# Order of weight sums, squares into PSUM, a last column block in two parts and closer turns in a one-core transformer block

## The chip, the cores and the metric

The kernel runs on one core of one Trainium2 chip. The core has TensorE (PE) for matmuls, VectorE (DVE), ScalarE (ACT), GpSimd (POOL) and SyncE (SP), which mostly issues DMAs. The metric is the device time of one execution in microseconds (us), taken as a median of several executions. A profile of one execution shows what each engine did and when.

## The reference

One layer on 256 tokens of width 2048, batch 1, all in fp32:

```
u = rms_norm(x);  z = u @ w_in          # 2048 -> hq hf hi hg | aq ak av | two gates
y_a = hgrn2_scan(silu(hq), 1-g, hi, log g), g = lb + (1-lb)*sigmoid(hf)   # 8 heads of 128, chunks of 64
y_a = rms_norm(y_a) * silu(hg)
y_b = attention over a band of 9 chunks with a relative bias              # 16 heads of 64
m = sigmoid(ga) * (y_a @ w_branch_a) + sigmoid(gb) * (y_b @ w_branch_b)
h = x + m @ w_out                       # 2048 x 2048
h = h + relu(rms_norm(h) @ w_up)**2 @ w_down   # 2048 -> 8192 -> 2048
out = rms_norm(h)
```

## The kernel before

**Matmuls.** Each fp32 product is three matmuls in a reduced form (`mm3`, L142 to L145): high part of the left times high part of the weight (L143), high times low (L144), low times high (L145). A weight piece of 128 x 1024 fp32 (512 KB) is loaded raw by SP (`piece`, L716), cast by ACT to its high part `wh` (L89) and subtracted by DVE to give the low part `wl` (L90). So PE waits for ACT and then DVE on each piece. A right-hand side has 512 columns at most; a PSUM bank holds 512 fp32 columns.

**HGRN stage.** The projections hf and hq are computed transposed (`gemm_t`, L171), the chunks hi and hg directly (`gemm`, L162). Beside these the small work of the recurrence is threaded through a list `behind` of steps with distances: each pass over a block of 128 rows of weights calls `tick` (L152), with 1 in `gemm_t` and 2 in `gemm`, and when the head step's distance is used up it is issued. `scores` (L517) puts eight steps per pair of heads on the list, the first of which, `diagonal`, makes the products `ps` (L373) from `q` (written by DVE at L338); its distance for pair 0 is 12. `group` (L535) puts on the list the outputs and then the turns of two pairs, the latter with distance `gap2`. A turn (`finish`, L491 on) transposes an output block on PE into a PSUM tile `tpo` (L493; the pool has two buffers), then ACT casts it and DVE subtracts (both into `act_ya`). The last step of attention's preparation before `ak` is `aq00T` (L193).

**Units.** Gates, output projection and the MLP run in units of 1024 output columns, two blocks of 512 (n = 0 and 1), for two row halves m: `Unit` (L758) and `run` (L854). The first half of the reduction is done with seven products of sums in place of eight (raw pieces A, B, C, D, each two tiles; sums of weights are made in place: A+B and A+C by DVE in `sums`, L816; B+C and D+A by accumulating DMAs from POOL in `sent`, L821). The sums of the left side, S2, S4, S5, S7, come from `combos` (L658; DVE at L679 to L685, then a split by ACT and DVE). The second half is plain pieces (`ITEMS`, L756). The last two pieces of column block 1 (`LATE`, k = 12, 13 and 14, 15) run inside the next unit, called by `q()` in `run`: one behind the next unit's first product, one behind its second. Names: `wl_wo2r` is the low part of a plain piece of unit wo2, `wl_up00p22A` that of piece A (by then A+B) in product 22 of unit up00. The units in order are ga2, gb0, gb2, (branch products), wo0, wo2, and then up00, up02, dn00, dn02 and so on to dn32.

**Order.** The scheduler of the framework puts each engine's instructions in an order of its own from the order in which they are written, with work under `high_priority` pulled ahead; what waits for what follows from buffers.

**Between wo2 and up00** `h_out` (L1031) adds x to the result; `h_blocks` (L1002) transposes it (`tp_h`, on PE at L106, in a pool of two PSUM buffers), multiplies by the norm's weight into `hw` (DVE, L1013), splits that into `act_h`, and takes the squares of h on ACT with a sum along the row (`hsq`, L1015) into a scratch tile in SBUF, a `token`; POOL's loads of x into such tokens (L1034) wait for tokens to come free.

**The end.** `out_of` (L1076) adds the result to h (`evict`, L753), takes squares on ACT (L1086), and with the last column block sums the squares, makes rstd (DVE L95, POOL L96), scales four blocks of 512 columns (i = 0 and 1 on ACT, 2 and 3 on DVE) and stores them, even i by ACT's queue, odd i by SP's.

Of the kernel before, what the change touches and what calls it, by code (L numbers as in the profile page):

```python
# [50 lines left out]
def tile_hybrid_block(  # L51
# [90 lines left out]
    def mm3(acc, hi, lo, wh, wl, first, last):  # L142
        nc.tensor.matmul(acc, hi, wh, start=first, stop=False, skip_group_check=True)  # L143
        nc.tensor.matmul(acc, hi, wl, start=False, stop=False, skip_group_check=True)  # L144
        nc.tensor.matmul(acc, lo, wh, start=False, stop=last, skip_group_check=True)  # L145
# [13 lines left out]
    def later(*steps):  # L159
        behind.extend([n, f] for n, f in steps)  # L160
# [356 lines left out]
    def scores(n, made, gap, first=None, between=()):  # L517

        sc = []
        steps = []  # L520

        def one(i):
            if not i:
                out, fs = hgrn_scores(n, made)
                sc.extend(out)
                steps.extend(fs)
            steps[i]()

        todo = [(gap if i or first is None else first, lambda i=i: one(i)) for i in range(8)]
        for at, f in between:  # L530
            todo.insert(at, (gap, f))
        later(*todo)
        return sc
# [13 lines left out]
    a0, a1 = fq(0), fq(1)  # L547
    a0[1]()
    a0[2]()
    s0 = scores(0, a0[0], 5, 12, ((5, a1[1]), (8, a1[2])))  # L550
    vs0 = v_chunk(0)
    s1 = scores(1, a1[0], 4)
    gws0 = hg_chunk(0)
# [6 lines left out]
    vs1 = v_chunk(1)  # L560
    s3 = scores(3, a3[0], 4)
    gws1 = hg_chunk(1)
    later(*group(1, s2, s3, vs1, gws1, 2, 3))
    acc_q = [gemm_t(xT, w_in_t, C_AQ + i * T, KD, f"aq0{i}") for i in range(2)]
    while behind:
        tick(9)
# [191 lines left out]
    class Unit:  # L758
# [64 lines left out]
        def plain(self, n, ks, which=range(NM)):  # L823

            while self.steps and self.steps[0][0] <= ks[-1] // 4:
                self.steps.pop(0)[1]()
            if (n, ks) not in self.raw:
                self.load_item()
            wh, wl = parts(self.raw[n, ks], f"{self.what}r{n}_{ks[0]}")

            def half(m):
                for a, k in enumerate(ks):
                    mm3(self.c["12"[m] + "12"[n]], *lhs_of(self.lhs(), k, m), wh[:, a], wl[:, a], False, k == KD - 1)

            for m in which:
                half(m)
            return half
# [16 lines left out]
    def run(u, then=None):  # L854

        def q():
            if late:
                late.pop(0)()

        def item(x):  # L860
            if x and x.items:
                x.load_item()

        if not u.raw:
            u.load("A")
            u.load("B")
            u.load("C")
            u.load("D")
        for _ in range(3 - sum(type(k) is tuple for k in u.raw)):
            item(u)  # L870
        at = iter(range(99))
        u.bank("11")
        u.product("11", "A", u.block(0, 0), True)
        u.sums("A", "B")
        u.begun("21", "11")
        u.sent("B", "C")
        q()
        item(u)
        u.bank("22")
        u.product("22", "A", u.comb(5), True)  # L880
        u.begun("12", "22")
        q()
        item(u)
        u.steps = list(u.make_steps())
        u.step(next(at))
        u.product("12", "C", u.comb(4))
        u.sums("A", "C")
        u.step(next(at))
        u.product("11", "D", u.block(0, 1))
        u.sent("D", "A")  # L890
        u.step(next(at))
        u.plain(1, (8, 9))
        item(u)
        u.step(next(at))
        u.product("21", "A", u.comb(2))
        u1 = u.copy(token(f"u1_{u.what}"), "21")
        if then:
            then.load("A")
        u.step(next(at))
        u.plain(1, (10, 11))  # L900
        u.less("12", u1)
        item(u)
        u.step(next(at))
        u.product("21", "B", u.comb(7))
        u2 = u.copy(token(f"u2_{u.what}"), "21")
        if then:
            then.load("B")
            then.load("C")
        u.step(next(at))
        u.plain(0, (8, 9))  # L910
        u.less("22", u2)
        item(u)
        u.step(next(at))
        u.plain(0, (10, 11))
        item(u)
        u.step(next(at))
        u.product("21", "D", u.block(1, 1))
        if then:
            then.load("D")
        u.step(next(at))  # L920
        u.plain(0, (12, 13))
        item(u)
        u.step(next(at))
        u.plain(0, (14, 15))
        item(then)
        u.end(0)
        while u.steps:
            u.step(99)

        if u.tail:  # L930
            halves = [u.plain(1, ks, ()) for ks in LATE]
            for m in range(NM):
                for h in halves:
                    h(m)
                u.done(m, 1, u.c["12"[m] + "2"])
            return

        def rest():
            u.plain(1, LATE[1])
            u.end(1)  # L940

        late.append(lambda: u.plain(1, LATE[0]))
        late.append(rest)
# [58 lines left out]
    def h_blocks(n0):  # L1002

        def one(n, m):
            if not m:
                hT.append(new_act(f"h{n}"))
            hi, lo = hT[n][:, :, 0, :], hT[n][:, :, 1, :]
            t = h1[n][m]
            tp = transpose4(t, f"h{n}{m}")
            tmp = fours(token(f"hw_{n}_{m}"))  # L1010
            hw[m, n] = tmp
            with tc.high_priority(offset=2000):
                nc.vector.tensor_tensor(tmp, tp, bc(wmlp[:, 4 * n:4 * n + 4], 2, P), op=ALU.mult)  # L1013
                split(hi[:, :, m * P:(m + 1) * P], lo[:, :, m * P:(m + 1) * P], tmp)
            nc.scalar.activation(token(f"hsq_{n}_{m}"), t, AF.Square, accum_out=ssq2[:, m, n:n + 1])  # L1015

        def factor():
            ssum2 = small.tile([P, NM], F32, name="ssum2", tag="ssum")
            nc.vector.tensor_reduce(ssum2, ssq2, axis=AX.X, op=ALU.add)
            rsqrt(rstd2, ssum2, D, NM)  # L1020

        def soon(f):
            with tc.high_priority(offset=2000):
                f()

        return [(n if n0 else 99, lambda n=n, m=m: one(n, m)) for n in (n0, n0 + 1) for m in range(NM)] + [
            (99, lambda f=f: soon(f), 6) for f in ([factor] if n0 else combos(hT, "h", sp, Sh, hw))]
# [8 lines left out]
        nc.gpsimd.dma_start(hd[n][m], t)  # L1036
        h1[n][m] = t

    ssq3 = small.tile([P, NM, 4], F32, name="ssq3", tag="ssq3")
    ssum3 = small.tile([P, NM], F32, name="ssum3", tag="ssum")  # L1040
    rstd3 = const.tile([P, NM], F32, name="rstd3")
    NQ = 4
# [3 lines left out]
    for qd in range(NQ):  # L1046
# [26 lines left out]
            units.append(Unit(lambda: hT, lambda: Sh, w_up, qd * (FF // NQ) + c * NC, f"up{qd}{c}", done,  # L1073
                              steps=(lambda turns=turns: turns(0)) if c else (lambda: ()) if qd else (lambda: h_blocks(2)), start=3 if c else 0))

        def out_of(m, n, acc, last=last, qd=qd):  # L1076
            if not last:
                t = token(f"y{qd}{n}{m}")
                with tc.high_priority(offset=2000):
                    nc.scalar.copy(t, acc)  # L1080
                nc.gpsimd.dma_start(hd[n][m], t, accum_op=ALU.add)
                return
            wf = fin["w"]
            r = fin[m][:, n * NC:(n + 1) * NC]
            evict(r, acc)
            nc.scalar.activation(token(f"ysq_{n}_{m}"), r, AF.Square, accum_out=ssq3[:, m, n:n + 1])  # L1086
            if n < 3:
                nc.vector.tensor_tensor(r, r, wf[:, n * NC:(n + 1) * NC], op=ALU.mult)
                return
            nc.vector.tensor_reduce(ssum3[:, m:m + 1], ssq3[:, m, :], axis=AX.X, op=ALU.add)  # L1090
            rsqrt(rstd3[:, m:m + 1], ssum3[:, m:m + 1], D, 1)
            f = rstd3[:, m:m + 1]
            for i in range(4):
                t = fin[m][:, i * NC:(i + 1) * NC]
                if i == 3:
                    nc.vector.scalar_tensor_tensor(t, t, f, wf[:, i * NC:(i + 1) * NC], op0=ALU.mult, op1=ALU.mult)
                elif i == 2:
                    nc.vector.tensor_scalar(t, t, f, None, op0=ALU.mult)
                else:
                    nc.scalar.activation(t, t, AF.Copy, scale=f)  # L1100
                (nc.sync if i % 2 else nc.scalar).dma_start(out[m * P:(m + 1) * P, i * NC:(i + 1) * NC], t)

        def finals():
            fin["w"] = apool.tile([P, D], F32, name="wf", tag="act")
# [5 lines left out]

        for n0 in (0, 2):
            units.append(Unit(lambda uT=uT: uT, lambda Su=Su: Su, w_down, n0 * NC, f"dn{qd}{n0}",
                              lambda m, n, acc, n0=n0, out_of=out_of: out_of(m, n0 + n, acc), kt0=qd * KD,
                              steps=(lambda: ()) if n0 else (lambda turns=turns, last=last: turns(2) + [(3, finals)] * last),
                              start=0, tail=last and n0 == 2))

# [46 lines left out]
```

## Time and profile before

| what | value |
|---|---|
| time, median of 3 runs | 1404.46 us (1403.69 to 1406.17) |
| the profiled execution's own time | 1403.92 us |
| its span, first to last instruction | 1402.2 us |
| mean granted TensorE clock | 0.998 |
| busy: PE, DVE, ACT, POOL | 99%, 80%, 65%, 10% of the span |
| moved by DMA | 327.42 MB, 234 GB/s on average |

The rows of the timeline give start and duration in us, engine, line, operation, tiles (out<-in), shape, and in brackets the idle time ahead of it with the instruction that ended it. A row of the waits gives engine, line and tile that waited, who ended the wait, total us, count and the longest. A row of the windows gives the stretch in us, its length, busy us of PE, PE's weight load, DVE, ACT and POOL with the number of instructions, the granted clock, the share of the DMA engines' time and GB/s.

### The profile page before, as it was taken

The numbers are of one execution on the slowest core, as the hardware profiler recorded it, in microseconds if no ns is written. First come the engines' busy times: TensorE is split into PE (matmuls) and PEld (weight loads), VectorE is DVE, ScalarE is ACT, GpSimd is POOL, SyncE is SP. The second block draws the span as 40 slices with busy tenths as digits, with TensorE's granted clock in tenths as the row PEclk, the third lists the DMA queues.
The fourth block names the chain that finished last, engine by engine and source line by source line (L and its number), as shares of the span: only waits on it lengthen the run. The fifth ranks groups of instructions, "written<-read, shape, count | busy, mean of one in ns | idle before, by whom it ended". The sixth has DMA issues, their size and how long they took to land.

```text
span 1402.2 us, 18580 instructions
## 1 busy us (share of the span) xinstructions
PE 1385.6 (99%) x6562; PEld 1149.9 (82%) x6562; DVE 1116.7 (80%) x1406; ACT 909.4 (65%) x1170; POOL 138.6 (10%) x220
## 2 busy tenths in 40 slices
PE   9999999999999999999999999999999999999997
PEld 8889888878787888888878888888888888888885
DVE  7897997675758785687998977889877897878885
ACT  6774754464656664446767876678666876668764
POOL 2000001010000000001211001100011001110200
PEclk9999999999999999999999999999999999999999
DMA  9654455555578987558988889988899888998883
GB/s 326 232 173 157 152 165 162 182 175 170 155 236 267 267 249 238 187 177 263 271 255 274 249 263 270 270 268 246 253 296 291 249 229 256 279 304 258 262 249 118
DMA packets 122925, 327.42 MB, mean 234 GB/s; under 512 B 10944, under 2 KB 11712, under 8 KB 122448
## 3 DMA queue, kind: packets, MB, share of 16 engines
q1 hardware_dynamic: 103264, 264.80, 55.3%
q0 software_dynamic: 18416, 59.84, 21.6%
q10 hardware_dynamic: 1152, 1.60, 0.3%
q8 instruction: 51, 0.84, 0.2%
q14 instruction: 42, 0.34, 0.1%
HBM read 271.67 MB, written 10.49 MB: 201 GB/s over the span
## 4 chain that ended last, share of the span: by engine, by line
PE 93%; DVE 2%; DMA 2%; issue 1%; ACT 1%; POOL 0%; ACTq 0%; POOLq 0%; DVEq 0%
PE acc_ak L185 2%; PE acc_aq L185 2%; PE acc_hf L185 1%; PE ps L417 1%; PE acc_hq L185 1%; PE acc_ga L144 1%; PE tp_u L106 1%; PE acc_ga L145 1%; PE acc_hg L143 1%; PE acc_hg L144 1%; PE acc_bb L143 1%; PE acc_ba L145 1%; PE acc_av L144 1%; PE acc_hg L145 1%; PE acc_ba L143 1%; PE acc_bb L145 1%
## 5 line engine op out<-in xcount | busy, mean ns | idle before, releaser
L185 PE MATMUL acc_hf<-act_x,wh_hf 128*128 128x512 f32 x128 | 46.3, 400 | 0.4 <-DVE f L193 0.4
L185 PE MATMUL acc_aq<-act_x,wh_aq 128*128 128x512 f32 x128 | 46.5, 400 | 0.0
L185 PE MATMUL acc_ak<-act_x,wh_ak 128*128 128x512 f32 x128 | 45.3, 399 | 0.7 <-DVE aq00T L193 0.7
L185 PE MATMUL acc_hq<-act_x,wh_hq 128*128 128x512 f32 x128 | 45.9, 397 | 0.0
L184 PE MATMUL acc_aq<-act_x,wl_aq 128*128 128x256 f32 x120 | 35.3, 294 | 0.0
L90 DVE TENSOR_TENSOR wl_ga<-raw_ga,wh_ga 128x1024 fp32r<-128x1024 f32 x16 | 19.6, 1225 | 19.6 <-ACT wh_ga L89 19.6
L184 PE MATMUL acc_hf<-act_x,wl_hf 128*128 128x256 f32 x120 | 34.3, 286 | 0.0
L184 PE MATMUL acc_hq<-act_x,wl_hq 128*128 128x256 f32 x120 | 34.2, 285 | 0.0
L184 PE MATMUL acc_ak<-act_x,wl_ak 128*128 128x256 f32 x120 | 33.7, 281 | 0.0
L90 DVE TENSOR_TENSOR wl_av<-raw_av,wh_av 128x1024 fp32r<-128x1024 f32 x16 | 19.6, 1224 | 16.7 <-ACT wh_av L89 16.7
L89 ACT CAST wh_bb<-raw_bb 128x1024 fp32r<-128x1024 f32 x16 | 16.8, 1053 | 23.3 <-PE acc_ba L145 17.8
L90 DVE TENSOR_TENSOR wl_bb<-raw_bb,wh_bb 128x1024 fp32r<-128x1024 f32 x16 | 19.6, 1224 | 14.8 <-ACT wh_bb L89 14.8
L89 ACT CAST wh_av<-raw_av 128x1024 fp32r<-128x1024 f32 x16 | 16.8, 1051 | 21.5 <-PE acc_av L145 12.4
L89 ACT CAST wh_ba<-raw_ba 128x1024 fp32r<-128x1024 f32 x16 | 16.8, 1051 | 20.9 <-PE acc_bb L145 13.8
L90 DVE TENSOR_TENSOR wl_aq<-raw_aq,wh_aq 128x1024 fp32r<-128x1024 f32 x16 | 19.6, 1224 | 13.4 <-ACT wh_aq L89 13.3
L90 DVE TENSOR_TENSOR wl_ba<-raw_ba,wh_ba 128x1024 fp32r<-128x1024 f32 x16 | 19.6, 1224 | 12.5 <-ACT wh_ba L89 12.5
L185 PEld LDWEIGHTS acc_ak<-act_x,wh_ak 128*128 128x128 f32 x128 | 24.0, 188 | 6.6 <-DVE aq00T L193 1.0
L89 ACT CAST wh_aq<-raw_aq 128x1024 fp32r<-128x1024 f32 x16 | 16.8, 1047 | 19.1 <-PE acc_hg L145 9.3
L185 PEld LDWEIGHTS acc_hf<-act_x,wh_hf 128*128 128x128 f32 x128 | 24.2, 189 | 5.7 <-DVE f L193 0.7
L185 PEld LDWEIGHTS acc_aq<-act_x,wh_aq 128*128 128x128 f32 x128 | 24.1, 189 | 5.2 <-issue 0.7
L89 ACT CAST wh_ga<-raw_ga 128x1024 fp32r<-128x1024 f32 x16 | 16.8, 1050 | 17.6 <-PE acc_ga L145 10.8
L185 PEld LDWEIGHTS acc_hq<-act_x,wh_hq 128*128 128x128 f32 x128 | 24.1, 188 | 5.0
(1806 smaller groups left out, 5249.9 us busy)
## 6 DMA issues: line engine op xcount, KB each, us to landing
raw_hi<-in_w_in_n_dram SPq DMA_DIRECT2D x16, 512.0 KB, 4.3
raw_hg<-in_w_in_n_dram SPq DMA_DIRECT2D x16, 512.0 KB, 3.8
raw_aq<-in_w_in_t_dram SPq DMA_DIRECT2D x16, 512.0 KB, 4.0
raw_ak<-in_w_in_t_dram SPq DMA_DIRECT2D x16, 512.0 KB, 3.8
raw_av<-in_w_in_n_dram SPq DMA_DIRECT2D x16, 512.0 KB, 4.3
raw_ga<-in_w_in_t_dram SPq DMA_DIRECT2D x16, 512.0 KB, 3.8
raw_ba<-in_w_branch_a_dram SPq DMA_DIRECT2D x16, 512.0 KB, 4.5
raw_bb<-in_w_branch_b_dram SPq DMA_DIRECT2D x16, 512.0 KB, 4.6
```

The lines of the kernel that those rows point to most:

```text
L89: (copy or nc.scalar.copy)(hi, src)
L90: nc.vector.tensor_tensor(lo, src, hi.bitcast(F32), op=ALU.subtract)
L106: nc.tensor.transpose(tp[:, j, :], src[:, j * P:(j + 1) * P], ident)
L143: nc.tensor.matmul(acc, hi, wh, start=first, stop=False, skip_group_check=True)
L144: nc.tensor.matmul(acc, hi, wl, start=False, stop=False, skip_group_check=True)
L145: nc.tensor.matmul(acc, lo, wh, start=False, stop=last, skip_group_check=True)
L184: nc.tensor.matmul(acc[:, cb, 0:T], wl[:, c], r[:, 0, :], start=False, stop=False)
L185: nc.tensor.matmul(acc[:, cb, :], wh[:, c], r.rearrange("p u t -> p (u t)"), start=kt == 0, stop=kt == nkt - 1)
L417: nc.tensor.matmul(ps[:, m, :], klf[:, a * P:(a + 1) * P], qrf[:, a * 192:(a + 1) * 192], start=True, stop=True)
```

## The change

Five edits:

- HGRN: the first diagonal of pair 0 has distance 13 in place of 12, and the turns of group 1 distance 2 in place of 3.
- In each unit the late piece (`q()`) is written ahead of the sum A+B, and the sum A+C behind the product with D.
- The squares of h are written into the PSUM tile of the transposes in place of a token.
- The last column block of the last unit, row half 1, is computed as two blocks of 256 columns, each with its own eviction and squares. The sums of squares get a fifth column.
- The outputs are scaled and stored in the order 2, 0, 3, 1, with 2 and 3 on SP's queue and 0 and 1 on ACT's.

```diff
-    s0 = scores(0, a0[0], 5, 12, ((5, a1[1]), (8, a1[2])))
+    s0 = scores(0, a0[0], 5, 13, ((5, a1[1]), (8, a1[2])))
...
-    later(*group(1, s2, s3, vs1, gws1, 2, 3))
+    later(*group(1, s2, s3, vs1, gws1, 2, 2))
...
-            def half(m):
+            def half(m, c=slice(0, NC)):
                 for a, k in enumerate(ks):
-                    mm3(self.c["12"[m] + "12"[n]], *lhs_of(self.lhs(), k, m), wh[:, a], wl[:, a], False, k == KD - 1)
+                    mm3(self.c["12"[m] + "12"[n]][:, c], *lhs_of(self.lhs(), k, m), wh[:, a, c], wl[:, a, c], False, k == KD - 1)
...
         u.product("11", "A", u.block(0, 0), True)
+        u.begun("21", "11")
+        q()
         u.sums("A", "B")
-        u.begun("21", "11")
         u.sent("B", "C")
-        q()
         item(u)
...
         u.product("12", "C", u.comb(4))
-        u.sums("A", "C")
         u.step(next(at))
         u.product("11", "D", u.block(0, 1))
+        u.sums("A", "C")
         u.sent("D", "A")
...
-            for m in range(NM):
+            for m, c in ((0, slice(0, NC)), (1, slice(0, T)), (1, slice(T, NC))):
                 for h in halves:
-                    h(m)
-                u.done(m, 1, u.c["12"[m] + "2"])
+                    h(m, c)
+                u.done(m, 1, u.c["12"[m] + "2"], c)
...
-            nc.scalar.activation(token(f"hsq_{n}_{m}"), t, AF.Square, accum_out=ssq2[:, m, n:n + 1])
+            nc.scalar.activation(tp.rearrange("p k t -> p (k t)"), t, AF.Square, accum_out=ssq2[:, m, n:n + 1])
...
-            evict(r, acc)
-            nc.scalar.activation(token(f"ysq_{n}_{m}"), r, AF.Square, accum_out=ssq3[:, m, n:n + 1])
+            evict(r[:, c], acc[:, c])
+            j = n + (c.start > 0)
+            nc.scalar.activation(token(f"ysq_{j}_{m}")[:, c], r[:, c], AF.Square, accum_out=ssq3[:, m, j:j + 1])
...
+            if c.stop < NC:
+                return
-            nc.vector.tensor_reduce(ssum3[:, m:m + 1], ssq3[:, m, :], axis=AX.X, op=ALU.add)
+            nc.vector.tensor_reduce(ssum3[:, m:m + 1], ssq3[:, m, 0:j + 1], axis=AX.X, op=ALU.add)
...
-            for i in range(4):
+            for i in (2, 0, 3, 1):
...
-                (nc.sync if i % 2 else nc.scalar).dma_start(out[m * P:(m + 1) * P, i * NC:(i + 1) * NC], t)
+                (nc.sync if i > 1 else nc.scalar).dma_start(out[m * P:(m + 1) * P, i * NC:(i + 1) * NC], t)
```

More of the change, by code (lines that the diff above doesn't have):

```diff
@@ L1037, in h_out @@
         h1[n][m] = t
-    ssq3 = small.tile([P, NM, 4], F32, name="ssq3", tag="ssq3")
+    ssq3 = small.tile([P, NM, 5], F32, name="ssq3", tag="ssq3")
     ssum3 = small.tile([P, NM], F32, name="ssum3", tag="ssum")
@@ L1074, in tile_hybrid_block, with out_of @@
                               steps=(lambda turns=turns: turns(0)) if c else (lambda: ()) if qd else (lambda: h_blocks(2)), start=3 if c else 0))
-        def out_of(m, n, acc, last=last, qd=qd):
+        def out_of(m, n, acc, c=slice(0, NC), last=last, qd=qd):
             if not last:
@@ L1112, in tile_hybrid_block @@
             units.append(Unit(lambda uT=uT: uT, lambda Su=Su: Su, w_down, n0 * NC, f"dn{qd}{n0}",
-                              lambda m, n, acc, n0=n0, out_of=out_of: out_of(m, n0 + n, acc), kt0=qd * KD,
+                              lambda m, n, acc, *c, n0=n0, out_of=out_of: out_of(m, n0 + n, acc, *c), kt0=qd * KD,
                               steps=(lambda: ()) if n0 else (lambda turns=turns, last=last: turns(2) + [(3, finals)] * last),
```

## The prediction

> **What bounds the kernel now.** I read the page first: busy shares, then the chain that ended last.
>
> ```profile
> span 1402.2 us, 18580 instructions
> PE 1385.6 (99%) x6562; PEld 1149.9 (82%) x6562; DVE 1116.7 (80%) x1406; ACT 909.4 (65%) x1170; POOL 138.6 (10%) x220
> PE 93%; DVE 2%; DMA 2%; issue 1%; ACT 1%; POOL 0%; ACTq 0%; POOLq 0%; DVEq 0%
> ```
>
> TensorE (PE) is busy for 1385.6 of 1402.2 us, and 93% of the chain of work that ended last is PE. The change removes no full-rate matmul work, so it can only win gaps: 16.6 us in all, most of them the load at the start and the output at the end. The waits of PE name the gaps inside.
>
> ```profile
> PE acc_wo2c L144 <- DVE wl_wo2r L90: 2.1, 2, 1.1
> PE acc_ga2c L144 <- DVE wl_ga2p11D L90: 1.0, 1, 1.0
> PE acc_ak L185 <- DVE aq00T L193: 0.7, 1, 0.7
> PE ps L373 <- DVE q L338: 0.5, 1, 0.5
> PE tpo L493 <- DVE act_ya L90: 0.4, 1, 0.4
> ```
>
> These five are 4.7 us. The timeline makes each a little longer, since a matmul still counts as busy when the next could have started: full ones start 0.227 us apart (0.23 in the first two rows below), so a gap is what exceeds that. DVE ends every one of the five, so what decides is DVE's order, which here I take from the instruction lists of the two kernels on each engine.
>
> **Part 1, first diagonal of HGRN pair 0 one tick later (12 to 13).**
>
> ```profile
> 60.76 0.39 PE L145 MATMUL acc_hi<-wh_hi,act_x 128*128 128x512 f32 x1
> 60.99 0.39 PE L143 MATMUL acc_hi<-wh_hi,act_x 128*128 128x512 f32 x1
> 61.92 0.92 PE L373 MATMUL ps<-q,kk 128*128 128x192 f32 x4 [0.54 <-DVE q L338]
> 63.38 0.81 PE L373 MATMUL ps<-q,kk 128*128 128x192 f32 x4
> ...
> 61.58 0.28 DVE L338 TENSOR_TENSOR q<-q,f 128x128 f32<-128x128 f32 x1
> 62.91 0.28 DVE L338 TENSOR_TENSOR q<-q,f 128x128 f32<-128x128 f32 x1
> ```
>
> The gap before the first ps is 61.92 − 60.99 − 0.227 = 0.70 us. The diagonal moves two matmuls down, 0.45 us, which leaves 0.25. But the second ps needs the second q, for which DVE still has a wl_hi to do first; that q ends at 63.19. The second ps starts at 63.25 instead of 63.38: **gain 0.13** (bounds 0 and 0.70).
>
> **Part 2, everything behind that diagonal is one tick later; here the turns of group 0.**
>
> ```profile
> 158.34 0.40 PE L145 MATMUL acc_hi<-wh_hi,act_x 128*128 128x512 f32 x1
> 159.18 0.44 PE L493 MATMUL tpo<-ident,o 128*128 128x128 f32 x2 [0.45 <-DVE act_ya L90]
> ...
> 148.93 0.16 DVE L95 TENSOR_SCALAR ms<-os 128x2 f32<-128x2 f32 x1
> 150.74 0.61 DVE L486 SCALAR_TENSOR_TENSOR o<-po,ro,gw 128x128 f32<-128x128 f32 x2 [0.52 <-POOL ro L96]
> 155.60 0.42 DVE L90 TENSOR_TENSOR act_ya<-tpo,act_ya 128x256 fp32r<-128x256 f32 x1
> 157.56 1.23 DVE L90 TENSOR_TENSOR wl_hi<-raw_hi,wh_hi 128x1024 fp32r<-128x1024 f32 x1
> 158.70 0.76 DVE L90 TENSOR_TENSOR act_ya<-tpo,act_ya 128x256 fp32r<-128x256 f32 x2
> ```
>
> The transposes tpo have two PSUM buffers, so the third turn waits until DVE has subtracted the first, and the fourth until the second. Before, the fourth loses 159.18 − 158.34 − 0.227 = 0.61. In the changed order DVE's subtraction for the **first** turn is no longer the row at 155.60; it stands behind the wl_hi of 157.56. Also, ms now comes behind the first wl_hi of the chunk, at about 151.85, and o follows ms by 1.65 us (148.93 + 0.16 to 150.74) through POOL, so o is at 153.5 and wl_hi at 157.85. The subtraction ends at 157.85 + 1.23 + 0.3 = 159.4. The third turn would start at 157.67 (two of the three earlier pairs and three matmuls of hi ahead of it): a gap of 1.8, after which the fourth has none. **Loss 1.8 − 0.6 = 1.15** (bounds: 0.3 if DVE takes the subtraction earlier by the idle time it has while it waits for POOL; 1.9).
>
> **Part 3, last turns of group 1 (distance 3 to 2).**
>
> ```profile
> 239.01 0.40 PE L185 MATMUL acc_aq<-act_x,wh_aq 128*128 128x512 f32 x1
> 240.07 0.50 PE L185 MATMUL acc_ak<-act_x,wh_ak 128*128 128x512 f32 x1 [0.66 <-DVE aq00T L193]
> 239.34 0.68 DVE L193 TENSOR_TENSOR aq00T<-acc_aq,aq00T 128x512 f32<-128x512 f32 x1
> ```
>
> The gap is 0.83. Turns done earlier take act_ya out of DVE's way ahead of aq00T. But the third turn now asks for its buffer while DVE is in a wl (about 0.26 of new gap), and the fourth 0.1. **Gain 0.3** (bounds 0 and 0.83).
>
> **Part 4, A+C of ga2 behind D.** In the changed order of every engine ga2 is as before: DVE takes the sums ahead of wl_p11D there. **Nothing**, and the 1.0 stays.
>
> **Part 5, wo2 to up00: A+B behind the late piece, squares in PSUM.**
>
> ```profile
> 710.73 0.39 PE L143 MATMUL acc_wo2c<-wh_wo2r,act_m 128*128 128x512 f32 x1
> 712.13 0.50 PE L144 MATMUL acc_wo2c<-wl_wo2r,act_m 128*128 128x512 f32 x1 [1.01 <-DVE wl_wo2r L90]
> 719.00 0.50 PE L144 MATMUL acc_wo2c<-wl_wo2r,act_m 128*128 128x512 f32 x1 [1.14 <-DVE wl_wo2r L90]
> ...
> 702.43 0.62 ACT L89 CAST S_h<-hw 128x512 fp32r<-128x512 f32 x1 [0.47 <-DVE hw L679]
> 706.65 1.05 ACT L89 CAST wh_wo2r<-rawp_wo2r 128x1024 fp32r<-128x1024 f32 x1 [3.60 <-DMA rawp_wo2r<-in_w_out_dram]
> ...
> 710.86 1.22 DVE L90 TENSOR_TENSOR wl_wo2r<-rawp_wo2r,wh_wo2r 128x1024 fp32r<-128x1024 f32 x1
> 718.86 2.36 DVE L90 TENSOR_TENSOR wl_up00p22A<-raw_up00A,wh_up00p22A 128x1024 fp32r<-128x1024 f32 x2
> ```
>
> The root is a weight transfer: ACT's cast waits for it until 706.65, and everything behind it on ACT and DVE waits too. The transfers there are bandwidth-bound, so moving the loads of x (their buffers no longer wait for the squares) shifts no bytes from behind this transfer to ahead of it:
>
> ```profile
> 700.00:706.00 6.00, 6.00 (x28) 4.86 (x28) 6.00 (x10) 2.58 (x4) 0.00 (x0) 1.00 1.03 377
> 711.00:745.00 34.00, 31.85 (x147) 25.99 (x147) 34.00 (x38) 24.50 (x34) 6.63 (x9) 1.00 0.85 236
> ```
>
> (DMA share 1.03 from 700 to 706; I allow 0.4 us earlier.) From 706.65 I follow DVE. The cast of S5 (702.43 before) now stands behind that cast, so it ends at 708.25 (706.65 + 1.05 + 0.6), and DVE has S5, L684, S7 and L685 from there (0.6 each, as the 128x512 forms), then wl_wo2r, ready at 711.85 against 712.08: gain 0.23. Two more S splits, wl_up00p11A twice, and the wl_wo2r of the second gap, now ahead of the sums, ready at 716.5: that gap, 1.30 from start to start as the first is 712.13 − 710.73 − 0.227 = 1.17 (0.16 over the 1.01 and 1.14 in the rows), goes. Next are two evictions (0.6 each) and two sums (1.14 each); wl_up00p22A is ready at 721.1 where PE wants it at 720.2, its second half, now behind the last wl_wo2r, at 723.4 where PE wants it at 722.5. Two gaps of 0.9 take the place of one of 1.3. PE is then at 724.5 instead of 724.35. The second row of the windows shows why little can be won: DVE is busy 34.00 of 34 us there, and what it does behind the transfer has grown by S5, L684 and L685 (1.8 us; a start 0.5 earlier and 0.2 less waiting between S casts take 0.7 off). So it runs 1.1 us later through the whole stretch, where the next wl_up00r has 0.84 us to spare (ends 733.29, used 734.13 below): another 0.2.
>
> ```profile
> 733.47 0.60 PE L106 MATMUL tp_h<-ident,h 128*128 128x128 f32 x4
> 734.13 0.40 PE L144 MATMUL acc_up00c<-wl_up00r,act_h 128*128 128x512 f32 x1
> 732.07 1.22 DVE L90 TENSOR_TENSOR wl_up00r<-rawp_up00r,wh_up00r 128x1024 fp32r<-128x1024 f32 x1
> 728.23 0.63 ACT L1015 ACTIVATE hsq<-h 128x512 f32<-128x512 f32 x1
> ```
>
> The squares cost the same 0.63 us, but now hold the PSUM tile, so the transposes two turns on wait for ACT as well. For the one at 733.47 the square is done about 731: hidden. If ACT were 2.6 us later it would show. **Part 5: loss 0.4** (bounds: gain 2.5, both gaps; loss 1.5). Between the other up and down units there is no gap to win; wl_p22A is ready over 3 us ahead there and loses about 1.1 of that: nothing.
>
> **Part 6, the end.**
>
> ```profile
> 1391.86 0.39 PE L145 MATMUL acc_dn32c<-wh_dn32r,act_u 128*128 128x512 f32 x1
> 1394.63 0.16 DVE L1090 TENSOR_REDUCE ssum<-ssq 128x1 f32<-128x4 f32 x1 [0.79 <-ACT ysq L1086]
> 1396.82 0.83 SPq L1101 DMA_DIRECT2D out_dram<-fin  x2
> ```
>
> Twelve matmuls of 512 columns become 12 + 12 of 256, about 0.117 us each (estimate: half of 0.227 and a little), the second dozen behind DVE's eviction of the first half: both halves lie in one PSUM tile, and the changed order shows PE waiting there. The twelve now end at 1392.25 (the last row of PE) and start 12 × 0.227 before 1392.1. First block from 1389.37 to 1390.94, eviction 0.42 (as the 128x256 act_ya) to 1391.40, second to 1393.05, 0.8 later than now. Its eviction and square are half as long, so the sum of squares comes at 1394.5, 0.1 sooner. The new order of outputs issues SP's last DMA at about 1396.8 instead of 1397.25: **gain 0.75** in all (bounds 0.2 and 1.4).
> The Trainium skill (PSUM — Partial Sum Buffer, Terms) says that two engines must not touch one PSUM bank at once, which speaks against splitting a column block inside one bank. No row here tests it. By it the gap between the blocks stays, which is the sum above; without it the gain would be 1.4.
>
> **Sum** against the profiled execution (1403.92 us, of which 1.7 lie around the span): −0.13 + 1.15 − 0.3 + 0 + 0.4 − 0.75 = +0.4, so **1404.3 us**. The median of the runs, 1404.46, is 0.5 above the profiled one, as much as the sum itself; I leave 1404.3. A measurement tells about 0.2%, 2.8 us, from no change.
>
> **Rivals.**
> 1. *It does what it says*: the gaps at 61, 159, 240, 712 and 719 go (0.70 + 0.61 + 0.83 + 1.17 + 1.30) and the end gives 0.75: 5.4 us, 1398.5. For it: each names one DVE instruction that moves. Against: DVE is full in 711–745 and the order puts wl_hi ahead of act_ya. A half of it, 1401, is as likely as the whole. Chance 0.15, both.
> 2. *DVE's delay meets the new wait on ACT (slower)*: in up00 the square of the second transpose stands behind a cast that needs a free weight buffer; if DVE and ACT run not 1.1 but over 1.8 us late there, the fourth transpose, 0.7 us behind that square, waits, its products come late to DVE, and the stall feeds itself. Price: with part 2 and part 5 at their upper bounds +1.9 + 1.5 and no gain but the end's 0.75, +2.6; with a stall of the cast's 1.05 on top, +3.7: 1406.5 to 1407.6. Chance 0.12.
> 3. *The HGRN order costs nothing* (DVE takes act_ya in its idle time): −0.75, 1403.2. It lies within the forecast's own spread, 0.73 with it.
>
> **How the numbers follow.** The terms' bounds reach from −5.5 to +3.2 (−0.7 + 0.3 − 0.83 − 2.5 − 1.4, with 0.4 of an earlier transfer; 0 + 1.9 + 0 + 1.5 − 0.2); they are largely independent, so the forecast's own spread is about ±1.7. With the halves of the rivals the range is 1401.6 to 1406.4. Faster by over 0.2% needs under 1401.65: rival 1, 0.15. Slower needs over 1407.27: the upper half of rival 2 and part of its lower, 0.09. Else the same, 0.76.
>
> **What would show it.** The third tpo waits over 1 us at 158–160 for act_ya; ga2's wait of 1.0 stays; in wo2 one wait is left and two appear at wl_up00p22A; a gap of some 0.7 inside the last 24 matmuls; the last outputs 0.5–0.8 us closer to the last matmul. I am wrong if the weight transfer lands much before or after 706.6, if DVE's real waits let act_ya go sooner, or if the transposes of h wait for ACT.

## The result and the profile after

The changed kernel takes **1424.09 us** (median of 4 runs, 1423.81 to 1426.35) against 1404.56 (4 runs, 1403.69 to 1406.17): ratio 1.0141, 95% interval 1.0124 to 1.0159. That is 20 us slower, and 18 us above the upper end of the range that was forecast. The profiled execution took 1423.81 us; its mean granted clock is 0.998, as before.

From the page of the changed kernel, the span and the busy times:

```profile
span 1422.1 us, 18613 instructions
PE 1408.7 (99%) x6574; PEld 1153.3 (81%) x6574; DVE 1118.8 (79%) x1407; ACT 908.3 (64%) x1172; POOL 137.9 (10%) x220
```

Read against the page of before: the span grew by 19.9 us, PE's busy time by 23.1 (1408.7 − 1385.6), and PE's idle time fell by 3.2 (16.6 to 13.4). PE has only 12 instructions more, those of the split block. So the loss is no wait at all: the same matmuls take longer. The waits of PE in the changed kernel say the same from the other side:

```profile
PE tpo L493 <- DVE act_ya L90: 1.1, 1, 1.1
...
PE acc_ga2c L144 <- DVE wl_ga2p11D L90: 0.8, 1, 0.8
PE acc_dn32c L143 <- DVE ssum L1093: 0.5, 1, 0.5
...
PE acc_up00c L144 <- DVE wl_up00p22A L90: 0.2, 1, 0.2
```

The third transpose, ga2, the gap inside the last block and wl_up00p22A are there as forecast, none of them long; the waits at wl_wo2r are gone. Nothing in this list is worth 20 us.

Where the time goes is seen from the first start of one matmul of a unit, in both kernels (from the trace by tile): the first of wo0 at 634.12 before and 8.22 us later after, of the first down unit at 801.73 and 8.91 later, of the last down unit at 1303.13 and 18.66 later. From the first unit of wo2 to the first down unit it stands still, since the two waits at wl_wo2r (2.1 us before) go there. Through the units of up and down it grows by 9.75 us in 501, though the diff changes there only the place of the late piece and the order in which weight sums are made. The timeline of the first down unit, before:

```profile
839.23 0.39 PE L144 MATMUL acc_dn00c<-wl_dn00r,act_u 128*128 128x512 f32 x1
...
841.27 0.39 PE L144 MATMUL acc_dn00c<-wl_dn00r,act_u 128*128 128x512 f32 x1
```

and after:

```profile
848.54 0.40 PE L143 MATMUL acc_dn00c<-wh_dn00r,act_u 128*128 128x512 f32 x1
...
850.40 0.39 PE L145 MATMUL acc_dn00c<-wh_dn00r,act_u 128*128 128x512 f32 x1
```

Nine steps in 2.04 us before are 0.227 us each; eight in 1.86 after are 0.2325. Over the whole trace, the spacing of two full matmuls in a row that have no S tile among them is on average 0.2269 before (3757 pairs) and 0.2325 after (3753): 0.0056 more, 21 us in all. Not every full matmul is touched alike. The view by tile, with durations in ns (minimum, median, maximum) and the first and last start, for two kinds of product in one down unit; before:

```profile
L144 PE MATMUL acc_dn02c<-wl_dn02p22A,S_u x4: 389/389/390, 850.1 to 852.2; 128*128 128x512 f32 x4
...
L144 PE MATMUL acc_dn02c<-wl_dn02r,act_u x32: 389/389/390, 861.0 to 895.7; 128*128 128x512 f32 x32
```

and after:

```profile
L144 PE MATMUL acc_dn02c<-wl_dn02p22A,S_u x4: 389/389/389, 859.9 to 862.0; 128*128 128x512 f32 x4
...
L144 PE MATMUL acc_dn02c<-wl_dn02r,act_u x32: 390/393/404, 871.0 to 906.4; 128*128 128x512 f32 x32
```

With a sum S_u on the left this matmul lasts 389 ns in both kernels; with act_u on the left its median goes from 389 to 393 and it varies. Two full matmuls in a row with S tiles on the left start 0.2272 us apart on average before (911 pairs) and 0.2287 after (909): little is lost there, and where it is, as in the products 12C and 21B of this unit, it is the first seven spacings of the twelve matmuls that are off (0.224 to 0.236), behind matmuls with act_u; the next four are 0.226 to 0.227 again.

One more kind loses nothing: the transposed projections of the HGRN stage and of attention, which have the weights on the left and act_x on the right. One matmul of 256 columns and one of 512 take 0.358 us together before and 0.357 after (some 450 pairs each).

What do S tiles and weights share, and act tiles not? In the addresses that the build gives each tile per partition, the fifth column of ssq3 makes that tile 40 bytes instead of 32. Each of its four buffers then takes 64 bytes instead of 32, so its pool (`small`) is 128 bytes longer, and everything that is laid out behind it moves up by 128: all weight tiles (wh from 111872 to 112000) and the S tiles (S5 from 167168 to 167296). The act tiles lie in a pool ahead of it and stay (the first at 20224). The distance from an act tile to a weight was a multiple of 256 bytes (91648 = 358 × 256); now it is half of 256 off. Between S and weights it is what it was.

**Theory A**: the distance between the addresses of the two operands sets the matmul's pace (act tile on the left, weights on the right), and the whole 20 us are that; the five edits do about what was forecast. **Theory B**: one of the edits (the order, the extra PSUM writer, the earlier x loads) slows PE, through traffic or order. **Theory C**: it is the address of the weights alone that matters, say its alignment.

### The profile page after: what moved, and what is told of

Same layout as the page of the kernel before. It is cut to its first block, busy times and chain, and to the rows that moved or that the text cites. A ratio compares the mean times of both kernels' runs of the same rounds, so it can differ in the third digit from the quotient of the medians.

```text
span 1422.1 us, 18613 instructions
## 1 busy us (share of the span) xinstructions
PE 1408.7 (99%) x6574; PEld 1153.3 (81%) x6574; DVE 1118.8 (79%) x1407; ACT 908.3 (64%) x1172; POOL 137.9 (10%) x220
## 4 chain that ended last, share of the span: by engine, by line
PE 94%; DVE 3%; DMA 1%; issue 1%; ACT 1%; POOL 0%; SPq 0%; POOLq 0%; DVEq 0%; ACTq 0%
PE acc_ak L185 2%; PE acc_aq L185 2%; PE acc_hf L185 2%; PE acc_hq L185 2%; PE ps L417 1%; PE acc_ga L144 1%; PE acc_ba L143 1%; PE acc_av L143 1%; PE acc_bb L144 1%; PE acc_bb L143 1%; PE acc_av L144 1%; PE acc_hg L145 1%; PE acc_ga L145 1%; PE acc_hg L143 1%; PE acc_bb L145 1%; PE acc_ba L144 1%
## 5 line engine op out<-in xcount | busy, mean ns | idle before, releaser
L90 DVE TENSOR_TENSOR wl_ba<-raw_ba,wh_ba 128x1024 fp32r<-128x1024 f32 x16 | 19.6, 1224 | 13.6 <-ACT wh_ba L89 13.6
```

Of the source, the lines that this page charges most:

```text
L90: nc.vector.tensor_tensor(lo, src, hi.bitcast(F32), op=ALU.subtract)
```

## Experiments

### The fifth column alone, and the change without its shift

The kernel before, with a fifth column that nobody uses (no instruction differs):

```diff
-    ssq3 = small.tile([P, NM, 4], F32, name="ssq3", tag="ssq3")
+    ssq3 = small.tile([P, NM, 5], F32, name="ssq3", tag="ssq3")
...
-            nc.vector.tensor_reduce(ssum3[:, m:m + 1], ssq3[:, m, :], axis=AX.X, op=ALU.add)
+            nc.vector.tensor_reduce(ssum3[:, m:m + 1], ssq3[:, m, 0:4], axis=AX.X, op=ALU.add)
```

> The kernel before with one edit: the tile ssq3 gets 5 columns, of which 4 are used as before. No instruction changes; the tile's pool grows by 128 B in each partition (four buffers, each rounded up from 32 to 64 B), and every tile of the weight pool and of the pools behind it moves up by 128 B, while the activations (pool ahead of it) stay. Theory A (addresses: matmuls whose stationary operand is an activation tile and whose moving operand is a weight tile lose some 5 ns when the two are 128 B apart in place of 0, modulo 512 B): about 1424 us, spacing of full matmuls 0.231 to 0.232 where act_ tiles are stationary and 0.227 where S tiles are. Theory B (the new order of instructions, or the program's 12 more matmuls, slows PE everywhere): 1404.5 us, spacing 0.227.

The changed kernel with two buffers of ssq3 (2 × 64 = 4 × 32 bytes), so that every other tile is back at its old address:

```diff
-    ssq3 = small.tile([P, NM, 5], F32, name="ssq3", tag="ssq3")
+    ssq3 = small.tile([P, NM, 5], F32, name="ssq3", tag="ssq3", bufs=2)
```

> The changed kernel with one edit: ssq3 has two buffers in place of four, so that its pool has the size that it had before and all tiles of weights and sums lie at their addresses of before. Order of instructions as in the changed kernel. Theory A (addresses): the spacing is back at 0.227 and the time is what the five edits give by themselves; with the gaps that the changed kernel's trace shows (at 158, 429, 730 and 1411 us) that is 1402 to 1404 us. Theory B (order or number of instructions): 1424 us.

Measured: the column alone takes 1425.33 us, 1.0151 times the kernel before (1.0136 to 1.0166), as slow as the whole change. The change at the old addresses takes 1403.19, ratio 0.9997 (0.9988 to 1.0006): no difference. The same two rows of the view by tile, of the kernel with the column alone:

```profile
L144 PE MATMUL acc_dn02c<-wl_dn02p22A,S_u x4: 389/389/389, 859.9 to 861.9; 128*128 128x512 f32 x4
...
L144 PE MATMUL acc_dn02c<-wl_dn02r,act_u x32: 390/393/404, 871.0 to 906.4; 128*128 128x512 f32 x32
```

They are the rows of the changed kernel, start times included to 0.1 us. Theory B falls: no edit of an instruction is needed for the 20 us, and with all of them they are gone.

### An unused tile that moves the weights

The kernel before, with an unused tile of 32 bytes in `small`, which moves the weights and S tiles, and no tile of the sums of squares changed:

```diff
+    small.tile([P, 8], F32, name="pad", tag="pad", bufs=1)
     room = small.tile([P, 40], F32, name="room", tag="room", bufs=1)
```

> The kernel before with an unused tile of 32 B ahead of the weight pool: weights lie 32 B further from the activations, modulo 512 B. No instruction changes. Theory A in its simplest form (any distance other than 0 costs): about 1424 us. If what counts is a coarser grain (64 or 128 B): 1404.5 us. Theory B: 1404.5 us.

The same with 256 bytes ([P, 64]):

> The kernel before with an unused tile of 256 B ahead of the weight pool: weights 256 B further, modulo 512 B. No instruction changes. Theory A: another time than at 128 B and at 0, if the cost comes from two reads of one memory whose places drift against each other; 0.227 or below is as possible as 0.232 (a full matmul has 512 columns, and the shortest spacings in the trace of before are 0.212 to 0.214, so up to 5% faster would be the far end, 1340 us; a repeat at 256 B would give 1404.5). Theory B: 1404.5 us.

And 128 bytes that move act tiles, weights and S tiles together:

```diff
     mhalf = const.tile([P, 32], F32, name="mhalf")
+    const.tile([P, 32], F32, name="pad")
```

> The kernel before with an unused tile of 128 B in the first pool: activations, weights and sums all move up by 128 B, so that their distance stays 0 modulo 256 B while every one of them now starts at 128 modulo 256. No instruction changes. If the distance between the stationary and the moving operand counts: 1404 us, spacing 0.227. If each tile's own place against a grain of 256 B counts: 1425 us, spacing 0.231 to 0.232.

Measured: 32 bytes 1427.77 us (1.0173, 1.0154 to 1.0191); 256 bytes 1403.34 (0.9993, 0.9984 to 1.0002); 128 bytes of everything 1404.07 (1.0005, 0.9995 to 1.0015). The tile rows of the last (its lines are one higher, for the added line):

```profile
L145 PE MATMUL acc_dn02c<-wl_dn02p22A,S_u x4: 389/389/389, 850.5 to 852.5; 128*128 128x512 f32 x4
...
L145 PE MATMUL acc_dn02c<-wl_dn02r,act_u x32: 389/389/389, 861.4 to 896.1; 128*128 128x512 f32 x32
```

Here the weights lie at 112000, as in the changed kernel, and the matmuls take 389 ns. Theory C falls: it is not where the weights are, but how far they are from the act tiles. The S tiles, too, lie here where they lie with the column alone, and two S matmuls in a row are back at 0.2271 us from 0.2286. So the little that is lost with S on the left is not a matter of its own two operands either; in the runs here it is there only where the act tiles are off.

Three more distances, one run each, beside 1403.37 of the kernel before: 64, 96 and 192 bytes ([P, 16], [P, 24] and [P, 48] in the line above).

> The kernel before, weights 64 B further from the activations. If every distance that is no multiple of 256 B costs the same: 1424 to 1428 us, spacing 0.231 to 0.233. If the cost has a pattern within 256 B: another value, below 0.227 not excluded.

> The kernel before, weights 96 B further from the activations. As with 64 B: 1424 to 1428 us if every distance that is no multiple of 256 B costs the same, else a point of the pattern.

> The kernel before, weights 192 B further from the activations (64 B short of the next multiple of 256 B). As with 64 B: 1424 to 1428 us if every distance that is no multiple of 256 B costs the same; if the pattern is not symmetric, another value than at 64 B.

The whole series (weights moved against the act tiles, in bytes):

| moved by | 0 | 32 | 64 | 96 | 128 | 192 | 256 |
|---|---|---|---|---|---|---|---|
| us | 1403.8 | 1427.77 | 1413.90 | 1428.91 | 1425.33 | 1429.30 | 1403.34 |
| mean spacing, act on the left, us | 0.2269 | 0.2333 | 0.2291 | 0.2334 | 0.2325 | 0.2334 | 0.2269 |
| mean spacing, S on the left, us | 0.2272 | 0.2273 | 0.2276 | 0.2299 | 0.2286 | 0.2295 | 0.2272 |

Zero and 256 cost nothing, 64 costs about 10 us, and the others 21 to 26. The spacings, over some 3700 pairs of act matmuls in each trace, follow the times, also where there is one run. The step from 0 to 32 already costs 24 us, so it isn't a slope, and 64 shows that it isn't a plain yes or no either. (No two full matmuls of the kernel before start less than 0.224 us apart; the 0.212 to 0.214 in the expectation for 256 bytes are the warm-up products of 128 columns at the start.)

### The steps of the prediction on the old addresses

The changed kernel on the old addresses lets the prediction's own steps be compared with the kernel before. Two more single steps undone in it: the squares of h back in a token, and the first diagonal back at distance 12 (both keep `bufs=2`).

```diff
-            nc.scalar.activation(tp.rearrange("p k t -> p (k t)"), t, AF.Square, accum_out=ssq2[:, m, n:n + 1])
+            nc.scalar.activation(token(f"hsq_{n}_{m}"), t, AF.Square, accum_out=ssq2[:, m, n:n + 1])
```

> The changed kernel with ssq3 at two buffers (addresses of before), and the squares of h back in a scratch tile in SBUF. That separates two of the edits at the end of wo2: the order of the sums stays, the casts and splits of the S tiles go back ahead of the late weight piece. If the squares in PSUM are what pushed S5 behind that piece: the gaps at 710, 719 and 722 us (0.73, 0.92, 0.78 in the run with the old addresses) shrink to the one at 710 (1.2) and small ones at up00p22A, in all 1 us less, 1402 to 1403.5 us. If the new order of the sums made them: no change, 1403.2 us.

```diff
-    s0 = scores(0, a0[0], 5, 13, ((5, a1[1]), (8, a1[2])))
+    s0 = scores(0, a0[0], 5, 12, ((5, a1[1]), (8, a1[2])))
```

> The changed kernel with ssq3 at two buffers (addresses of before), and the first diagonal at distance 12 as before. The gap of the turns at 157 us should go back from 1.29 to 0.6, and the one before the first ps from 0.25 to 0.70: by the prediction's parts 1 and 2 a gain of 0.3 to 1.0 us, 1402.2 to 1402.9 us; if the turns' wait does not hang on that distance, no change, 1403.2 us.

And a version put together from what these suggest: `bufs=2`, distance 12, squares in a token, and the loads of x for the column blocks after the second on SP's queue, behind the weights, without priority:

```diff
-        with tc.high_priority(offset=2000):
-            nc.gpsimd.dma_start(t, x[m * P:(m + 1) * P, n * NC:(n + 1) * NC])
+        with tc.high_priority(offset=0 if n > 1 else 2000):
+            (nc.sync if n > 1 else nc.gpsimd).dma_start(t, x[m * P:(m + 1) * P, n * NC:(n + 1) * NC])
```

> The edits that the traces speak for, put together: late piece ahead of the sums, turns of group 1 at distance 2, the end of the changed kernel, addresses of before; first diagonal at 12 and squares in a scratch tile as before; and new, the four last loads of x go by SP's queue behind the late weight piece of wo2 in place of POOL's ahead of it, so that this piece, on which ACT, DVE and PE wait at 706 us, has 1 MB less ahead of it (1 MB at the 377 GB/s of that stretch is 2.8 us). If that transfer sets the gaps at 710 to 722: they go, 2.4 us, and with 0.3 to 0.7 from the diagonal and 0.4 at the end 1400.5 us, ratio 0.998. If the DVE chain behind it sets them: 1402.5 us. If the loads of x come too late for the additions at 715: slower, 1405.

Measured on one chip: old token 1402.27 us (0.9991, 0.9982 to 1.0000), old distance 1403.34 (0.9993, 0.9984 to 1.0002), put together **1401.64** (0.9984, 0.9975 to 0.9993). The last is the only one whose interval lies below 1; it is 2.5 us faster than the kernel before beside it (1404.14), and 1.1 us above the 1400.5 that was expected if the transfer sets the gaps. The old token came out as expected. The old distance did not in time (1402.2 to 1402.9 was expected), though both its gaps went back as expected. Against the old-token version the difference of 0.6 us is too small to count as shown.

Squares in a token: ACT's timeline from 701 to 706 of that kernel,

```profile
701.90 0.62 ACT L89 CAST S_h<-hw 128x512 fp32r<-128x512 f32 x1 [0.47 <-DVE hw L679]
705.67 1.05 ACT L89 CAST wh_wo2r<-rawp_wo2r 128x1024 fp32r<-128x1024 f32 x1 [3.14 <-DMA rawp_wo2r<-in_w_out_dram]
```

against that of the changed kernel on the old addresses, further down, where the cast of S5 stands behind the late weight piece. From the first start of wo2's product 11A to that of up00's 21D, PE is 1.2 us faster than in the kernel before; with the squares in PSUM it was 0.28 slower. So this one edit costs 1.5 us there. The runs don't part its two effects: S5's cast comes behind the late piece, and the four loads of x (256 KB each) are issued from 685.97 on, not from 692.09 (by the timeline), into queues that are full; the weight piece ahead of the late one is cast at 701.75 with the early loads and at 700.38 without.

Old distance: the timeline of PE at the turns of group 0, where the loss of 0.6 is back that the kernel before has at that place,

```profile
158.11 0.40 PE L145 MATMUL acc_hi<-wh_hi,act_x 128*128 128x512 f32 x1
158.95 0.44 PE L493 MATMUL tpo<-ident,o 128*128 128x128 f32 x2 [0.44 <-DVE act_ya L90]
...
233.47 0.39 PE L185 MATMUL acc_aq<-act_x,wh_aq 128*128 128x512 f32 x1
234.59 0.44 PE L493 MATMUL tpo<-ident,o 128*128 128x128 f32 x2 [0.73 <-DVE act_ya L90]
```

and 0.7 before the first ps (60.76) with it, and a new one of 0.89 at 233.47, the third turn of group 1. Its ratio to the kernel before (0.9993) is that of distance 13 (0.9997) within the intervals, and the same stretch from wo2 to up00, untouched by that edit, came out 0.5 us longer here, so differences of half a microsecond between these versions are not told apart.

Put together: ACT's casts of the same stretch, and then the windows' row for 711 to 745,

```profile
702.51 0.62 ACT L89 CAST S_h<-hw 128x512 fp32r<-128x512 f32 x1 [0.30 <-DVE hw L679]
703.58 1.06 ACT L89 CAST wh_wo2r<-rawp_wo2r 128x1024 fp32r<-128x1024 f32 x1 [0.45 <-DMA rawp_wo2r<-in_w_out_dram]
```

```profile
711.00:745.00 34.00, 34.00 (x160) 28.13 (x159) 33.88 (x39) 23.92 (x33) 8.44 (x9) 1.00 0.90 251
```

The four loads of x are now issued from 700.60 to 703.32 (692.44 to 698.63 before), behind the weights, and land behind the late piece, at 706.61 and later. The late weight piece is there at 703.58, where it came at 706.65 in the kernel before and at 705.67 with the old token alone, and PE is busy 34.00 of 34 us (31.85 before). Both gaps at wl_wo2r are gone and none takes their place: from wo2 to up00 2.8 us are won. Not all of it reaches the time of this execution (1402.38, the slowest of its 11): from PE's last matmul of 512 columns to the end of the span it took 13.6 us, where the changed kernel on the old addresses took 12.6, with the same end.

## Why the prediction was wrong

**The step that failed** is an unwritten one under the first part: "The change removes no full-rate matmul work, so it can only win gaps", with "full ones start 0.227 us apart" taken over for the changed kernel. No term of the sum, no bound and no rival allowed an instruction that is not touched to take another time. The fifth column of ssq3 stands in the change and had no term; alone it was +21.5 us (1425.33 against 1403.80), where the whole change was +19.5. Sum and rivals were all about waits, and the list of waits does not hold this loss.

**The five edits themselves** came out close to their terms in sum, two of them by another way than was forecast. The waits of PE in the changed kernel on the old addresses:

```profile
PE acc_up00c L144 <- DVE wl_up00p22A L90: 1.4, 2, 0.8
PE tpo L493 <- DVE act_ya L90: 1.1, 1, 1.1
...
PE acc_ga2c L144 <- DVE wl_ga2p11D L90: 1.0, 1, 1.0
PE acc_wo2c L144 <- DVE wl_wo2r L90: 0.6, 1, 0.6
...
PE acc_dn32c L143 <- DVE ssum L1093: 0.5, 1, 0.5
```

and its timeline, where the terms are read:

```profile
62.70 0.92 PE L373 MATMUL ps<-q,kk 128*128 128x192 f32 x4 [0.19 <-DVE q L338]
...
156.91 0.40 PE L145 MATMUL acc_hi<-wh_hi,act_x 128*128 128x512 f32 x1
158.43 0.41 PE L493 MATMUL tpo<-ident,o 128*128 128x128 f32 x2 [1.12 <-DVE act_ya L90]
...
229.41 0.39 PE L185 MATMUL acc_aq<-act_x,wh_aq 128*128 128x512 f32 x1
230.10 0.46 PE L475 MATMUL po<-v,so 128*128 128x128 f32 x2 [0.29 <-DVE o L486]
...
239.43 0.39 PE L185 MATMUL acc_aq<-act_x,wh_aq 128*128 128x512 f32 x1
239.81 0.50 PE L185 MATMUL acc_ak<-act_x,wh_ak 128*128 128x512 f32 x1
...
710.55 0.39 PE L143 MATMUL acc_wo2c<-wh_wo2r,act_m 128*128 128x512 f32 x1
711.51 0.50 PE L144 MATMUL acc_wo2c<-wl_wo2r,act_m 128*128 128x512 f32 x1 [0.57 <-DVE wl_wo2r L90]
...
719.59 0.39 PE L143 MATMUL acc_up00c<-wh_up00p22A,S_h 128*128 128x512 f32 x1
720.73 0.50 PE L144 MATMUL acc_up00c<-wl_up00p22A,S_h 128*128 128x512 f32 x1 [0.76 <-DVE wl_up00p22A L90]
...
722.00 0.40 PE L143 MATMUL acc_up00c<-wh_up00p22A,S_h 128*128 128x512 f32 x1
723.00 0.50 PE L144 MATMUL acc_up00c<-wl_up00p22A,S_h 128*128 128x512 f32 x1 [0.61 <-DVE wl_up00p22A L90]
...
1390.71 0.28 PE L145 MATMUL acc_dn32c<-wh_dn32r,act_u 128*128 128x256 f32 x1
1391.51 0.39 PE L143 MATMUL acc_dn32c<-wh_dn32r,act_u 128*128 128x256 f32 x1 [0.52 <-DVE ssum L1093]
...
151.22 0.16 DVE L95 TENSOR_SCALAR ms<-os 128x2 f32<-128x2 f32 x1
152.42 0.61 DVE L486 SCALAR_TENSOR_TENSOR o<-po,ro,gw 128x128 f32<-128x128 f32 x2 [0.58 <-POOL ro L96]
156.73 1.22 DVE L90 TENSOR_TENSOR wl_hi<-raw_hi,wh_hi 128x1024 fp32r<-128x1024 f32 x1
157.86 0.75 DVE L90 TENSOR_TENSOR act_ya<-tpo,act_ya 128x256 fp32r<-128x256 f32 x2
...
706.22 1.05 ACT L89 CAST wh_wo2r<-rawp_wo2r 128x1024 fp32r<-128x1024 f32 x1 [2.80 <-DMA rawp_wo2r<-in_w_out_dram]
707.18 1.14 ACT L89 CAST S_h<-hw 128x512 fp32r<-128x512 f32 x2
```

(This execution reached the first diagonal 0.56 us earlier than the one of before, a difference of the start; starts are compared with that taken out.)

| part | forecast, us | measured, us | from |
|---|---|---|---|
| 1, first diagonal | −0.13 | −0.12 | second ps at 62.70 + 0.56 against 63.38 |
| 2, turns of group 0 | +1.15 | +0.68 | gap 158.43 − 156.91 − 0.227 = 1.29, against 0.61 |
| 3, turns of group 1 | −0.3 | −0.22 | 0.15 ahead of ak and 0.46 at 229.41, against 0.83 |
| 4, ga2 | 0 | 0 | the wait of 1.0 stays |
| 5, wo2 to up00 | +0.4 | +0.28 | from the first start of wo2's 11A to that of up00's 21D |
| 6, the end | −0.75 | −0.43 | from PE's matmul at 1389.17 (1389.14 before) to the end of the span (1401.8, 1402.2) |
| sum | +0.4 | +0.2 | |

The measured column is of one execution of each kernel. The medians of the runs differ by −0.6 us, with an interval from −1.7 to +0.8, so they neither show the sum nor speak against it.

Part 2 was right in place and cause, and too dear: the subtraction does stand behind wl_hi, but ms came at 151.22 (forecast 151.85), o began 1.04 after ms had ended and not 1.65, and wl_hi came at 156.73 (157.85): with the 0.56 of the start put back, the last is still 0.56 ahead of the forecast. Part 3 came near by luck: no turn of group 1 waits here (0.26 and 0.1 were forecast for the third and fourth), and the 0.46 is a wait of the product po for o (230.10), which no term had. At the old distance that wait is absent and the third turn waits 0.89, more than the 0.83 that was to be won, so there the closer turns gain nothing. Part 5 went as followed through: S5's cast (707.18, two casts in the row) behind the late piece, one wait at wl_wo2r instead of two (the first gap 711.51 − 710.55 − 0.227 = 0.73 instead of 1.17), and two gaps of 0.91 and 0.77 at wl_up00p22A, forecast as 0.9 each. The late piece was there at 706.22, 0.4 earlier, as was allowed. Part 6: the gap between the blocks is 0.68 as forecast (0.7); less was won behind it. The sum of squares was to come 0.1 sooner and did not (1394.70 against 1394.63 before), and the last output is issued at 1397.08, not 1396.8, against 1397.25 before; it lands at 1400.70 against 1400.78. The rest of the 0.43 lies behind the last landing (1.07 us to the end of the span, 1.43 before), where no term looked for it. Of the rivals, the first (it does what it says, 1398.5) is out, since the gaps at 159, 240, 712 and 719 all have a successor; the second (DVE meets the new wait on ACT) did not occur: no transpose of h is in the list; the third (HGRN's order costs nothing) was off by 0.3, the sum of parts 1 to 3.

What the prediction said of the loads of x ("shifts no bytes from behind this transfer to ahead of it") held against the kernel before, where the late piece came 0.4 later (706.65), but against the same kernel with the old token it is 0.5 later (706.22, 705.67). And the loads were ahead of it in the kernel before too: all four landed by 706.23 and the piece at 706.55, though three of them were issued after it, on another queue. Put behind it, with the old token and the old distance, the stretch gains 2.8 us, against 1.2 with the old token alone; some 1.6 of it is then the loads' (the half microsecond between like versions taken into account, 1 to 2). The DMA share of 1.03 said that the transfers are full; what can be changed there is their order.

What stays open is the mechanism of the pace. The runs show that it goes by the distance between the act tile on the left and the weights on the right, and not how. Nor do they show why the same distance costs nothing in the transposed projections, and whether that is for the side on which the weights stand or for the shapes.

## What to carry to other kernels

When a change moves the time by a per cent or more and the list of waits doesn't hold it, compare the spacing of one kind of matmul in both traces before anything else, and then the addresses of its two operands. Where a change touches the size or the number of buffers of any tile, however small, look at which tiles move and which stay; an unused tile of the missing bytes, or fewer buffers, puts them back, and without that an edit's own effect isn't seen. A list of instructions that is the same in two kernels does not make their times the same.

## What was not expected of the hardware

- A matmul with an act tile on the left and 128 x 512 weights on the right starts 0.227 us after the one ahead of it when the operands lie a multiple of 256 bytes apart, and 0.2325 on average when they are 128 off, with the granted clock at 0.998 in both; in the unit shown its duration goes from a steady 389 ns to between 390 and 404.
- The Trainium skill (TensorE: Matmul & The Clock Gate, Step-by-step: what each phase is for) says that TensorE has two independent read ports, so that loading the next tile's weights takes no read bandwidth from the running matmul. That gives no reason for a distance between the operands to matter; here it does, 1403.8 against 1425.3 us with not one instruction changed, and the measurement decides. Why it does, no run here shows.
- A tile that grew by 8 bytes moved the weights by 128, through the rounding of each of its four buffers from 32 to 64 bytes.
- A distance of 64 bytes costs about 10 us where 32, 96, 128 and 192 cost 21 to 26 (64, 96 and 192 with one run each).
